# Attention with two key tiles per operation in two double-bank PSUM buffers

## The chip, the cores and the metric

The kernel runs on one core of a Trainium2 chip. Its time is the device time of one launch in microseconds (us); a kernel stands for the median of its runs. TensorE (PE) multiplies matrices into PSUM, VectorE (DVE), ScalarE (ACT) and GpSimd (POOL) do the rest, SyncE (SP) issues most DMAs. Each engine takes its instructions in a fixed order and waits at each for what it needs.

## The reference

One encoder layer on 2048 + 256 tokens of width 1024. The input is normed and projected; eight mLSTM heads and eight attention heads (two key/value heads, head width 64) run side by side; their outputs are projected and added, and a gated feed-forward layer with a width-3 convolution follows. The part that the change touches is the attention:

```python
s = jnp.einsum('bqhgd,bkhd->bhgqk', qi, k).astype(jnp.float32) * scale
p = jax.nn.softmax(s, axis=-1)
return jnp.einsum('bhgqk,bkhd->bqhgd', p.astype(v.dtype), v)
```

Keys are those of the same request: 2048 for the long one, 256 for the short one.

## The kernel before

The program runs in stages: the projections for attention and gates, then attention and mLSTM woven together, then the output projection (`phase_c`, tile `po`), which is woven into the last part of attention, then the feed-forward layer.

**Attention** works in 36 blocks of 512 queries. A block is named by its first head and first query tile of 128: `7_12` is head 7, query tiles 12 to 15. Blocks `0_0` to `7_12` (32 of them) meet 2048 keys, which are 16 key tiles or 8 key pairs `kp`; the four blocks `0_16`, `2_16`, `4_16`, `6_16` belong to the short request and have one key pair. A block goes through these steps:

- `prep` (L494 on) transposes the queries into PSUM (`pq`) and copies them out twice (`qq`, `qm`).
- `maxstep` multiplies 128 queries with 512 keys into a tile `px` (L521), and DVE takes the row maxima (`mx`, L522). A block needs 16 such steps; they are done while the block before it is in its key pairs.
- `prep2` joins the maxima, turns them into a row with TensorE (`pr`, L533), and ACT writes it as row 64 of `qm` (L535), so that a second matmul subtracts the maximum.
- `scores`, for each key tile: two matmuls into `ps` (L544, L545), ACT takes the exponential (`pe`, L548) and copies it rounded into the first half of `xx` (L549), DVE writes the remainder into the second half (L550).
- `values`, two key pairs later (`PLAG`): three matmuls per key tile add into the block's one `pv` bank (L562 to L564). The third takes the remainder from DVE.
- `fin1` copies `pv` out on ACT (`o` L571, `rs` L572, 64 partitions by 512); `fin2` does four reciprocals on DVE (L578), one product on POOL (L579), and stores the block into `mix_d` through POOL's DMA queue (L582).

`px`, `ps`, `pq` and `pr` share one PSUM pool, tag `sc`, of four single-bank buffers (`SCB = 4`). The bank of `pv` has no second buffer. mLSTM has three banks of its own (`mj`/`mv`, and `m` twice).

**What sets the order.** The program is written down as generators that `run_both` draws from in turn by estimated costs; a list scheduler then fixes the order of each engine's instructions by priority and by when it expects each to be ready. So TensorE's order has attention, mLSTM projections and, from 1516 us of the span on, `po` matmuls mixed together. `po` for a group of 256 tokens can only be finished when all heads of those tokens are in `mix_d`: `phase_c` loads them as `cmx` (L918), splits them on ACT and DVE, and multiplies (L932). When attention has ended its buffers go to the feed-forward layer, which begins by loading and combining the normed input (`rn`, `n`, `nt`, L1005 to L1028).

Of the kernel before, what the change touches and what calls it, by code (L numbers as in the profile page):

```python
# [17 lines left out]
P = 128  # L18
# [11 lines left out]
ACOL = 2048  # L30
MPRI = 2000
STORE = "sync"
SCB = 4
MB = 2
MJ = 1
BLK = 768
# [5 lines left out]
NX0 = 2  # L42
NPC = 1
WSTEP = 2
MXE = 4
LASTP = 3
OW3 = 3
OTB = 3
# [20 lines left out]
RW = 4  # L69
PO = 4  # L70
PB = 4
PEB = 3
XB = 6
PLAG = 2
ZT = 3
SG = 3
# [353 lines left out]
def attention(g, tc, s1, s2, pp):  # L430
# [62 lines left out]
    def prep(n):  # L493

        s = HB()
        grp, s.qs, k0, k1 = hbs[n]
        load_q(n)
        load_q(n + 1)
        load_kv(grp, k0, k1)
        s.kv = kv[(grp, k0)]  # L500
        s.nq, s.nk = 4, k1 - k0
        s.N = s.nq * P
        s.nm = "%d_%d" % s.qs[0][0:2]
        qz = qzs.pop(n)
        pq = pp.tile([P, 512], F32R, tag="sc", name="pq" + s.nm)
# [6 lines left out]
        s.mx = sp.tile([P, 4, 4], F32, tag="mx", name="mx" + s.nm, bufs=2)  # L512
        s.nsp = -(-s.nk * P // 512)
        s.todo = [(t, z) for z in range(s.nsp) for t in range(s.nq)]
        return s

    def maxstep(s):
        t, z0 = s.todo.pop(0)
        w = min(512, s.nk * P - z0 * 512)
        ps = pp.tile([P, 512], F32, tag="sc", name=f"px{s.nm}_{t}_{z0}")  # L520
        nc.tensor.matmul(ps[:, 0:w], s.qq[:, t * P:(t + 1) * P], s.kv[z0][0][:, 0:w], start=True, stop=True)  # L521
        nc.vector.tensor_reduce(s.mx[:, t, z0:z0 + 1], ps[:, 0:w], AX.X, ALU.max)  # L522

    def prep2(s):

        nq = s.nq
        s.m4 = sp.tile([P, 4], F32, tag="m4", name="m4" + s.nm, bufs=2)
        nc.vector.tensor_reduce(s.m4[:, 0:nq], s.mx[:, 0:nq, 0:s.nsp], AX.X, ALU.max)
        m4r = sp.tile([P, 4], F32R, tag="m4r", name="m4r" + s.nm, bufs=2)
        nc.vector.tensor_scalar(m4r[:, 0:nq], s.m4[:, 0:nq], -1.0, None, ALU.mult)  # L530
        pr = pp.tile([P, 512], F32, tag="sc", name="pr" + s.nm)
        for t in range(nq):
            nc.tensor.matmul(pr[:, t * P:(t + 1) * P], m4r[:, t:t + 1].to_broadcast([P, P]), g.identr, start=True,  # L533
                             stop=True)
        nc.scalar.activation(s.qm[HD:HD + 1, 0:s.N], pr[HD:HD + 1, 0:s.N], AF.Copy)  # L535

    def scores(s, kp):
        N = s.N
        xs = []
        kk, kl1 = s.kv[kp // 2][0:2]  # L540
        for z in range(2):
            ps = pp.tile([P, 512], F32, tag="sc", name=f"ps{s.nm}_{kp}_{z}")
            kc = (2 * kp + z) % 4 * P
            nc.tensor.matmul(ps[:, 0:N], kk[:, kc:kc + P], s.qq[:, 0:N], start=True, stop=False)  # L544
            nc.tensor.matmul(ps[:, 0:N], kl1[:, kc:kc + P], s.qm[:, 0:N], start=False, stop=True)  # L545
            pe = sp.tile([P, 512], F32, tag="pe", name=f"pe{s.nm}_{kp}_{z}", bufs=PEB)
            x = sp.tile([P, 2, 512], F32R, tag="px", name=f"xx{s.nm}_{kp}_{z}", bufs=XB)
            nc.scalar.activation(pe[:, 0:N], ps[:, 0:N], AF.Exp)  # L548
            nc.scalar.activation(x[:, 0, 0:N], pe[:, 0:N], AF.Copy)  # L549
            nc.vector.tensor_tensor(x[:, 1, 0:N], pe[:, 0:N], f32(x[:, 0, 0:N]), ALU.subtract)  # L550
            xs.append(x)
        return kp, xs

    def values(s, kp, xs):

        N = s.N
# [3 lines left out]
        for z, x in enumerate(xs):  # L560
            kt = 2 * kp + z
            nc.tensor.matmul(s.pv[:, 0:N], vv[:, kt % 4, :], x[:, 0, 0:N], start=kt == 0, stop=False)  # L562
            nc.tensor.matmul(s.pv[0:HD, 0:N], vl[:, kt % 4, :], x[:, 0, 0:N], start=False, stop=False)  # L563
            nc.tensor.matmul(s.pv[:, 0:N], vv[:, kt % 4, :], x[:, 1, 0:N], start=False, stop=kt == s.nk - 1)  # L564

    def fin1(s):

        N = s.N
        s.o1 = sp.tile([HD, 512], F32, tag="o1", name="o1" + s.nm, bufs=2)
        s.rs = sp.tile([HD, 512], F32, tag="rs", name="rs" + s.nm, bufs=1)  # L570
        nc.scalar.activation(s.o1[:, 0:N], s.pv[0:HD, 0:N], AF.Copy)  # L571
        nc.scalar.activation(s.rs[:, 0:N], s.pv[HD:P, 0:N], AF.Copy)  # L572

    def fin2(s):
        N = s.N
        for t in range(s.nq):
            c = slice(t * P, (t + 1) * P)
            nc.vector.reciprocal(s.rs[:, c], s.rs[:, c])  # L578
        nc.gpsimd.tensor_tensor(s.o1[:, 0:N], s.o1[:, 0:N], s.rs[:, 0:N], ALU.mult)  # L579
        for t0, (h, q0, q1) in part(s):  # L580
            r0 = HD * (h % 2)
            nc.gpsimd.dma_start(g.mix_d[q0 // 2:q1 // 2, r0:r0 + HD, 4 + h // 2].rearrange("n p t -> p n t"),  # L582
                           s.o1[:, t0 * P:(t0 + q1 - q0) * P].rearrange("p (n t) -> p n t", t=BT))
            if h == 7:
                g.mixed.update(range(q0, q1))

# [961 lines left out]
```

## Time and profile before

| | |
|---|---|
| median of three runs | 3370.09 us (3361.63 to 3379.33) |
| profiled execution | 3368.61 us, of which 3366.9 us from its first to its last instruction |
| TensorE busy | 97% |
| DVE, ACT, POOL busy | 76%, 60%, 20% |
| mean granted TensorE clock | 0.989 |

Attention begins at about 256 us of the span and ends at about 1773 us. A row of the profile's groups names the line, the engine, the operation, output and input tiles, their shapes and the count; behind the bar stand the busy time in us, the mean duration of one in ns, and the idle time of the engine just before them with what ended it. PEld is TensorE's load of the stationary operand, which overlaps the matmul before it. A matmul's duration covers its passage through the array; the next one can start before it ends, so the distance between two starts is the better price.

### The profile page before, as it was taken

Reading aid. Unit: us, or ns where it says so; the run is one execution under the profiler, and the core shown is the slowest. Engines: PE = TensorE matmul, PEld = TensorE weight load, DVE = VectorE, ACT = ScalarE, POOL = GpSimd, SP = SyncE. Lnnn points to the kernel's source line nnn. Section 1 sums busy time; section 2 is a strip of 40 time slices with the busy share of each in tenths; the row PEclk is TensorE's granted clock in tenths of the full one; section 3 lists DMA queues with packets and bytes.
Section 4 is the critical chain, followed back from the end, with each engine's and each line's share of the span. In section 5 each row is a group of like instructions: output and inputs, shape, how many; then the busy total and the mean of one; then the engine's idle time right before and its main releaser. Section 6 shows DMA issues by size and latency. Waiting matters only on the chain.

```text
span 3366.9 us, 54718 instructions
## 1 busy us (share of the span) xinstructions
PE 3267.3 (97%) x19566; PEld 3033.5 (90%) x19566; DVE 2561.9 (76%) x4259; ACT 2015.5 (60%) x4154; POOL 686.9 (20%) x1040
## 2 busy tenths in 40 slices
PE   7989999999999999999999899999999999999998
PEld 6778888888888888878889899999999999999998
DVE  7875677768767887887775899998888888666663
ACT  4534667666666677666562555666666767554543
POOL 7775123213331332321112000000000000020201
PEclk9999999999999999999999999999999999999999
DMA  8756233333334443434237666668676657867663
GB/s 246 217 181 188 90 103 96 107 106 106 99 106 147 129 124 124 125 106 136 90 102 256 244 216 223 213 241 281 216 247 237 212 191 254 315 230 274 224 236 115
DMA packets 394048, 601.76 MB, mean 179 GB/s; under 512 B 30736, under 2 KB 255024, under 8 KB 393776
## 3 DMA queue, kind: packets, MB, share of 16 engines
q1 hardware_dynamic: 361232, 553.43, 49.2%
q0 software_dynamic: 11088, 33.04, 3.6%
q10 hardware_dynamic: 21456, 11.80, 1.2%
q8 instruction: 154, 2.52, 0.3%
q14 instruction: 118, 0.97, 0.1%
HBM read 434.23 MB, written 163.92 MB: 178 GB/s over the span
## 4 chain that ended last, share of the span: by engine, by line
PE 74%; DVE 7%; issue 5%; DMA 5%; POOL 4%; ACT 4%; SPq 0%; POOLq 0%; ACTq 0%; DVEq 0%
PE pa L1082 16%; PE pc L1082 8%; PE po L932 5%; PE pf L1338 5%; PE pb L1082 4%; PE mj L672 4%; PE mv L682 4%; PE ps L544 3%; PE ps L545 3%; PE pv L564 3%; PE px L521 3%; PE pv L562 3%; PE pv L563 3%; PE pg L1338 2%; PE ph L1338 2%
## 5 line engine op out<-in xcount | busy, mean ns | idle before, releaser
L550 DVE TENSOR_TENSOR xx<-pe,xx 128x512 fp32r<-128x512 f32 x520 | 371.7, 727 | 167.2 <-ACT xx L549 164.1
L548 ACT ACTIVATE pe<-ps 128x512 f32<-128x512 f32 x520 | 299.0, 596 | 153.7 <-PE ps L545 140.6
L522 DVE TENSOR_REDUCE mx<-px 128x1 f32<-128x512 f32 (+1 forms) x528 | 339.0, 669 | 51.3 <-PE px L521 50.0
L1296 POOL TENSOR_TENSOR sq<-sq,sq 128x384 f32<-128x384 f32 x38 | 48.8, 1284 | 1394.9 <-ACT sq L1292 1314.6
L549 ACT ACTIVATE xx<-pe 128x512 fp32r<-128x512 f32 x520 | 316.4, 633 | 4.7
L932 PEld LDWEIGHTS po<-cmx,wo 128*128 128x128 f32 x1728 | 231.5, 190 | 17.8 <-ACT wo L106 0.8
L932 PE MATMUL po<-cmx,wo 128*128 128x256 f32 x1728 | 241.5, 282 | 0.7 <-DVE cx L937 0.3
L1086 ACT ACTIVATE u<-pa 128x386 f32<-128x386 f32 (+2 forms) x264 | 129.2, 490 | 172.1 <-PE pa L1082 171.2
L564 PE MATMUL pv<-xx,vv 128*128 128x512 f32 x520 | 214.5, 413 | 12.3 <-DVE xx L550 12.1
L544 PE MATMUL ps<-qq,kk 128*128 128x512 f32 x520 | 214.3, 415 | 2.0 <-ACT pe L548 1.4
L562 PE MATMUL pv<-xx,vv 128*128 128x512 f32 x520 | 209.8, 403 | 2.3 <-ACT xx L549 1.1
L545 PE MATMUL ps<-qm,kl 65*128 65x512 f32 x520 | 208.5, 404 | 0.1
L563 PE MATMUL pv<-xx,vl 128*64 128x512 f32 x520 | 207.0, 398 | 0.0
L682 PE MATMUL mv<-wm,mn 128*128 128x256 f32 x1296 | 204.9, 287 | 1.9 <-ACT qb L678 1.9
L672 PE MATMUL mj<-mn,wm 128*128 128x256 f32 x1296 | 199.5, 287 | 6.8 <-ACT og L686 4.8
L672 PEld LDWEIGHTS mj<-mn,wm 128*128 128x128 f32 x1296 | 184.1, 191 | 23.7 <-ACT og L686 5.6
L682 PEld LDWEIGHTS mv<-wm,mn 128*128 128x128 f32 x1296 | 187.4, 191 | 18.9 <-ACT qb L678 2.5
L521 PE MATMUL px<-kk,qq 128*128 128x512 f32 (+1 forms) x528 | 199.1, 410 | 3.5 <-ACT qq L509 1.9
L227 PE MATMUL pj<-w_a,n1T 128*128 128x512 f32 (+1 forms) x864 | 178.6, 361 | 10.0 <-DVE n1T L185 6.6
L227 PEld LDWEIGHTS pj<-w_a,n1T 128*128 128x128 f32 x864 | 144.1, 196 | 30.4 <-DVE n1T L185 7.8
L776 ACT ACTIVATE dm<-dm,tm 128x128 f32<-128x128 f32 x288 | 95.7, 392 | 100.4 <-POOL dm L773 95.9
L1082 PE MATMUL pb<-n,wa 128*128 128x386 f32 (+2 forms) x792 | 147.1, 340 | 4.2 <-DVE cx L949 4.2
(322 smaller groups left out, 8375.3 us busy)
## 6 DMA issues: line engine op xcount, KB each, us to landing
mn<-n_d SPq DMA_DIRECT2D x216, 256.0 KB, 3.1
ru<-w_up SPq DMA_DIRECT2D x88, 512.0 KB, 5.1
rs<-wsu_d SPq DMA_DIRECT2D x88, 512.0 KB, 5.6
act_d<-ts SPq DMA_DIRECT2D x33, 768.0 KB, 5.8
nt<-act_d SPq DMA_DIRECT2D x60, 384.0 KB, 5.1
re_t<-wsd_d SPq DMA_DIRECT2D x45, 512.0 KB, 5.2
wsu_d<-tw SPq DMA_DIRECT2D x44, 512.0 KB, 3.6
act_d<-ya SPq DMA_DIRECT2D x99, 192.0 KB, 2.7
```

Of the source, the lines that this page charges most:

```text
L227: nc.tensor.matmul(pjs[t][:, c0:c1], nTs[tiles[t]][:, c, a, :], ws[c][:, b, c0:c1], start=(c == 0 and k == 0), stop=(c == NCC - 1 and k == 2))
L522: nc.vector.tensor_reduce(s.mx[:, t, z0:z0 + 1], ps[:, 0:w], AX.X, ALU.max)
L544: nc.tensor.matmul(ps[:, 0:N], kk[:, kc:kc + P], s.qq[:, 0:N], start=True, stop=False)
L545: nc.tensor.matmul(ps[:, 0:N], kl1[:, kc:kc + P], s.qm[:, 0:N], start=False, stop=True)
L549: nc.scalar.activation(x[:, 0, 0:N], pe[:, 0:N], AF.Copy)
L550: nc.vector.tensor_tensor(x[:, 1, 0:N], pe[:, 0:N], f32(x[:, 0, 0:N]), ALU.subtract)
L562: nc.tensor.matmul(s.pv[:, 0:N], vv[:, kt % 4, :], x[:, 0, 0:N], start=kt == 0, stop=False)
L564: nc.tensor.matmul(s.pv[:, 0:N], vv[:, kt % 4, :], x[:, 1, 0:N], start=False, stop=kt == s.nk - 1)
L672: nc.tensor.matmul(pj[:, o], s.w[c][:, a, o * P:(o + 1) * P], nT[c][:, h, :], start=(c + o + k == 0), stop=(c == NCC - 1 and k == 2 and o ...
L682: nc.tensor.matmul(pv[:, o], nT[c][:, a, o * P:(o + 1) * P], s.w[c][:, h, 256:512], start=(c + o + k == 0), stop=(c == NCC - 1 and k == 2 ...
L932: nc.tensor.matmul(po[:, o], wo[c][z // 2][:, a, n], mx[c][:, h, :], start=(c == 0 and k == 0), stop=(c == NCC - 1 and k == 2))
L1082: s.nc.tensor.matmul(p, w[:, aa, c, :], ops[k][:, c, bb, 0:s.n], start=c == 0 and i == 0 and not add, stop=c == NCC // 2 - 1 and i == 2, s ...
```

## The change

Attention's PSUM pool becomes two buffers of two banks each (`SCB = 2`, tiles of 1024 columns). Everything that goes through it changes shape:

- `maxstep` does two matmuls of 512 keys into one tile and one maximum over 1024 keys. A long block has 8 steps instead of 16. A short block does all four query tiles in one tile and one reduction.
- `scores` puts both key tiles of a pair into one tile by four matmuls; exponential, copy and remainder are one operation each over 1024 columns instead of two over 512.
- `values` reads the halves of the one `xx` tile; its six matmuls are as before.
- `fin1` copies `pv` in four pieces of 64 partitions by 256 columns so that `o1` and `rs` fill 128 partitions by 256; `fin2` then does two reciprocals instead of four, one product over 128 by 256, and two stores per long block instead of one.
- The buffers in SBUF follow: `pe` two of 1024 columns instead of three of 512, `xx` three instead of six. `MXE` goes from 4 to 2, and the table that spaces the maxima at the change of the key/value head is rewritten for 8 steps.

```diff
-SCB = 4
+SCB = 2
-MXE = 4
+MXE = 2
-PEB = 3
-XB = 6
+PEB = 2
+XB = 3
...
     def maxstep(s):
...
+            for z in range(2):
+                nc.tensor.matmul(ps[:, z * 512:(z + 1) * 512], s.qq[:, t0 * P:(t0 + 1) * P], s.kv[2 * z0 + z][0],
+                                 start=True, stop=True)
+            nc.vector.tensor_reduce(s.mx[:, t0, z0:z0 + 1], ps, AX.X, ALU.max)
...
     def scores(s, kp):
...
+        ps = pp.tile([P, 1024], F32, tag="sc", name=f"ps{s.nm}_{kp}")
         for z in range(2):
...
+            nc.tensor.matmul(o, kk[:, kc:kc + P], s.qq, start=True, stop=False)
+            nc.tensor.matmul(o, kl1[:, kc:kc + P], s.qm, start=False, stop=True)
+        pe = sp.tile([P, 1024], F32, tag="pe", name=f"pe{s.nm}_{kp}", bufs=PEB)
+        x = sp.tile([P, 2, 1024], F32R, tag="px", name=f"xx{s.nm}_{kp}", bufs=XB)
+        nc.scalar.activation(pe, ps, AF.Exp)
+        nc.scalar.activation(x[:, 0], pe, AF.Copy)
+        nc.vector.tensor_tensor(x[:, 1], pe, f32(x[:, 0]), ALU.subtract)
...
     def fin1(s):
...
-        nc.scalar.activation(s.o1[:, 0:N], s.pv[0:HD, 0:N], AF.Copy)
-        nc.scalar.activation(s.rs[:, 0:N], s.pv[HD:P, 0:N], AF.Copy)
+        for z in range(2):
+            for r, o in ((0, s.o1), (HD, s.rs)):
+                nc.scalar.activation(o[HD * z:HD * z + HD], s.pv[r:r + HD, 256 * z:256 * z + 256], AF.Copy)
 
     def fin2(s):
-        for t in range(s.nq):
+        for t in range(2):
...
-        nc.gpsimd.tensor_tensor(s.o1[:, 0:N], s.o1[:, 0:N], s.rs[:, 0:N], ALU.mult)
+        nc.gpsimd.tensor_tensor(s.o1, s.o1, s.rs, ALU.mult)
...
-                    k = 2 * (kp - 2) - (nxt.nq * nxt.nsp - len(nxt.todo))
+                    k = (0 if kp < 5 else 2 if kp == 5 else 4) - (nxt.steps - len(nxt.todo))
```

The scheduler gives every engine a new order. Three places of TensorE's order matter below. Names carry block, key pair and a running number; `po4_2` is the output projection of token group 4, `cmx6_7` the attended heads 6 and 7 of token group 6. The changed file is nine lines longer behind the attention, so L932 is L941 there; L544, L545 are L553, L554, and L562 to L564 are L570 to L572.

The first place is block `7_12`, key pairs 6 and 7. Before:

```order
L544 MATMUL ps7_12_6_0_21964<-qq7_12_21541,kk1_16_12_11639 128x512
L545 MATMUL ps7_12_6_0_21964<-qm7_12_21543,kl11_16_12_11640 128x512
L564 MATMUL pv7_12_21869<-xx7_12_4_0_21924,vv1_16_8_11630 128x512
L932 MATMUL po4_2_20832<-cmx4_3_20636,wo3_1_18739 128x256
L544 MATMUL ps7_12_6_1_21972<-qq7_12_21541,kk1_16_12_11639 128x512
L545 MATMUL ps7_12_6_1_21972<-qm7_12_21543,kl11_16_12_11640 128x512
L932 MATMUL po4_2_20832<-cmx4_3_20636,wo3_1_18739 128x256 x2
L544 MATMUL ps7_12_7_0_21986<-qq7_12_21541,kk1_16_12_11639 128x512
L545 MATMUL ps7_12_7_0_21986<-qm7_12_21543,kl11_16_12_11640 128x512
L932 MATMUL po4_2_20832<-cmx4_4_20640,wo4_1_18771 128x256
```

And with the change, from key pair 6 on:

```order
L553 MATMUL ps7_12_6_19929<-qq7_12_19612,kk1_16_12_10655 128x512
L554 MATMUL ps7_12_6_19929<-qm7_12_19614,kl11_16_12_10656 128x512
L572 MATMUL pv7_12_19874<-xx7_12_3_19887,vv1_16_4_10635 128x512
L570 MATMUL pv7_12_19874<-xx7_12_3_19887,vv1_16_4_10635 128x512
L571 MATMUL pv7_12_19874<-xx7_12_3_19887,vl1_16_4_10636 64x512
L572 MATMUL pv7_12_19874<-xx7_12_3_19887,vv1_16_4_10635 128x512
L570 MATMUL pv7_12_19874<-xx7_12_4_19903,vv1_16_8_10646 128x512
L571 MATMUL pv7_12_19874<-xx7_12_4_19903,vl1_16_8_10647 64x512
L553 MATMUL ps7_12_7_19945<-qq7_12_19612,kk1_16_12_10655 128x512
```

No `po` matmul stands there any more: mLSTM and `po` have moved ahead of attention, and from key pair 3 of block `6_12` to the last matmuls of `6_16` (168 rows of the order) attention is alone but for two `po` matmuls near the end.

The second place is the turn from block `6_12` to `7_12`, where `pv` changes hands. Before, the first matmul into the new `pv` stands 20 rows behind the last one into the old, with others of this kind in between:

```order
L564 MATMUL pv6_12_21618<-xx6_12_7_1_21765,vv1_16_12_11641 128x512
L129 MATMUL rs_c3_20710<-ones_82,cacc3_20147 128x2 x2
L521 MATMUL px4_16_1_0_21850<-kk1_2_0_21794,qq4_16_21810 128x256
L932 MATMUL po4_1_20756<-cmx4_0_20624,wo0_0_18708 128x256 x3
L932 MATMUL po4_1_20756<-cmx4_1_20628,wo1_0_18718 128x256 x3
L932 MATMUL po4_1_20756<-cmx4_2_20632,wo2_0_18728 128x256 x3
```

With the change it follows at once:

```order
L570 MATMUL pv6_12_19663<-xx6_12_7_19771,vv1_16_12_10657 128x512
L571 MATMUL pv6_12_19663<-xx6_12_7_19771,vl1_16_12_10658 64x512
L572 MATMUL pv6_12_19663<-xx6_12_7_19771,vv1_16_12_10657 128x512
L570 MATMUL pv7_12_19874<-xx7_12_0_19829,vv1_16_0_10624 128x512
L571 MATMUL pv7_12_19874<-xx7_12_0_19829,vl1_16_0_10625 64x512
```

The bank is the same; what lies between is `fin1`, which is ACT's.

The third place is the end of attention with the change, where `po` is taken up again:

```order
L543 MATMUL pr6_16_20009<-identr_78,m4r6_16_20007 128x128 x4
L553 MATMUL ps6_16_0_20201<-qq6_16_19984,kk1_2_0_19802 128x512
L554 MATMUL ps6_16_0_20201<-qm6_16_19986,kl11_2_0_19803 128x512
L553 MATMUL ps6_16_0_20201<-qq6_16_19984,kk1_2_0_19802 128x512
L554 MATMUL ps6_16_0_20201<-qm6_16_19986,kl11_2_0_19803 128x512
L570 MATMUL pv6_16_20270<-xx6_16_0_20207,vv1_2_0_19804 128x512
L571 MATMUL pv6_16_20270<-xx6_16_0_20207,vl1_2_0_19805 64x512
L941 MATMUL po6_0_20060<-cmx6_7_20052,wo7_0_17149 128x256
L941 MATMUL po6_1_20147<-cmx6_7_20052,wo7_0_17149 128x256
```

Before, `po` of group 5 stands between `pr6_16`, `ps6_16` and `pv6_16`. When attention's last matmul is issued, 1196 of the 1728 `po` matmuls have been issued with the change, and 1037 before it.

More of the change, by code (lines that the diff above doesn't have):

```diff
@@ L504, in prep @@
         qz = qzs.pop(n)
-        pq = pp.tile([P, 512], F32R, tag="sc", name="pq" + s.nm)
+        pq = pp.tile([P, 1024], F32R, tag="sc", name="pq" + s.nm)
         for t in range(s.nq):
@@ L511, in prep @@
         nc.scalar.activation(s.qm[0:HD, 0:s.N], f32(pq[0:HD, 0:s.N]), AF.Copy)
-        s.mx = sp.tile([P, 4, 4], F32, tag="mx", name="mx" + s.nm, bufs=2)
-        s.nsp = -(-s.nk * P // 512)
-        s.todo = [(t, z) for z in range(s.nsp) for t in range(s.nq)]
+        s.mx = sp.tile([P, 4, 2], F32, tag="mx", name="mx" + s.nm, bufs=2)
+        s.nsp = -(-s.nk * P // 1024)
+        s.todo = [(t, z) for z in range(s.nsp) for t in range(s.nq)] if s.nk * P > 512 else [(None, 0)]
+        s.steps = len(s.todo)
         return s
     def maxstep(s):
[L518 to L522, printed above, removed]
+        t0, z0 = s.todo.pop(0)
+        ps = pp.tile([P, 1024], F32, tag="sc", name=f"px{s.nm}_{t0}_{z0}")
+        if t0 is None:
+            w = s.nk * P
+            for t in range(s.nq):
+                nc.tensor.matmul(ps[:, t * w:(t + 1) * w], s.qq[:, t * P:(t + 1) * P], s.kv[0][0][:, 0:w], start=True,
+                                 stop=True)
+            nc.vector.tensor_reduce(s.mx[:, 0:s.nq, 0], ps[:, 0:s.nq * w].rearrange("p (t w) -> p t w", w=w), AX.X,
+                                    ALU.max)
+        else:
+            for z in range(2):
+                nc.tensor.matmul(ps[:, z * 512:(z + 1) * 512], s.qq[:, t0 * P:(t0 + 1) * P], s.kv[2 * z0 + z][0],
+                                 start=True, stop=True)
+            nc.vector.tensor_reduce(s.mx[:, t0, z0:z0 + 1], ps, AX.X, ALU.max)
     def prep2(s):
@@ L530, in prep2 @@
         nc.vector.tensor_scalar(m4r[:, 0:nq], s.m4[:, 0:nq], -1.0, None, ALU.mult)
[L531 removed]
+        pr = pp.tile([P, 1024], F32, tag="sc", name="pr" + s.nm)
         for t in range(nq):
```

40 lines of the change are left out of this document (15 added, 25 removed).

## The prediction

> **What bounds the kernel now.** I read the page first, then the busy time by stage, then what TensorE's weight loads waited for, then the groups of instructions. The page says that TensorE is the busy engine:
>
> ```profile
> span 3366.9 us, 54718 instructions
> PE 3267.3 (97%) x19566; PEld 3033.5 (90%) x19566; DVE 2561.9 (76%) x4259; ACT 2015.5 (60%) x4154; POOL 686.9 (20%) x1040
> ```
>
> By stage (columns: length, then busy time of each engine, granted clock, DMA share, GB/s) attention covers the first three rows, the rest of the output projection and the passage to the feed-forward layer the last two:
>
> ```profile
> 300.00:1000.00 700.00, 691.67 (x4317) 604.08 (x4316) 509.83 (x1071) 468.58 (x1217) 182.73 (x339) 0.99 0.34 104
> 1000.00:1600.00 600.00, 578.22 (x3498) 489.17 (x3497) 472.15 (x1040) 394.88 (x1015) 160.68 (x289) 0.99 0.41 126
> 1600.00:1776.00 176.00, 176.00 (x1165) 157.56 (x1164) 127.32 (x219) 102.28 (x196) 33.31 (x30) 1.00 0.29 95
> 1776.00:1860.00 84.00, 82.89 (x699) 82.43 (x698) 46.42 (x87) 21.69 (x38) 23.17 (x20) 1.00 0.83 279
> 1860.00:1890.00 30.00, 19.42 (x88) 17.66 (x87) 23.41 (x35) 10.10 (x15) 3.94 (x3) 0.83 0.89 304
> ```
>
> In the 1476 us of attention TensorE is idle for 8.3 + 21.8 + 0 = 30 us. DVE is busy for 1109 us (75%) and ACT for 966 us (65%), so neither bounds the stage. What they cost is how often TensorE waits for them. From 255 to 1790 us its weight loads waited like this (us in total, times, longest):
>
> ```profile
> PEld pv L564 <- DVE xx L550: 23.3, 29, 3.0
> PEld px L521 <- ACT pe L548: 4.4, 11, 1.2
> PEld pv L562 <- ACT xx L549: 4.0, 10, 1.0
> PEld ps L544 <- ACT pe L548: 3.4, 7, 1.2
> ...
> PEld px L521 <- DVE mx L522: 2.5, 7, 0.4
> ...
> PEld ps L544 <- DVE mx L522: 2.1, 7, 0.4
> ```
>
> Rows one and three are waits for results, 27.3 us; the other four are waits for a free PSUM buffer, 12.4 us. Together 39.7 us (1.2% of the time) is all that the attention can win by faster ACT and DVE steps.
>
> **The change part by part.** The sum is made against the profiled execution: 3368.61 us, 1.7 us over its span and 1.5 us below the median of the three runs.
>
> The ACT and DVE steps that are merged, and their prices (mean ns of one behind the bar):
>
> ```profile
> L550 DVE TENSOR_TENSOR xx<-pe,xx 128x512 fp32r<-128x512 f32 x520 | 371.7, 727 | 167.2 <-ACT xx L549 164.1 <-PE mv L682 0.6
> L522 DVE TENSOR_REDUCE mx<-px 128x1 f32<-128x512 f32 x512 | 333.0, 677 | 42.4 <-PE px L521 41.2
> L549 ACT ACTIVATE xx<-pe 128x512 fp32r<-128x512 f32 x520 | 316.4, 633 | 4.7
> L548 ACT ACTIVATE pe<-ps 128x512 f32<-128x512 f32 x520 | 299.0, 596 | 153.7 <-PE ps L545 140.6 <-DVE mx L522 4.0 <-DVE xx L550 2.0
> ...
> L578 DVE RECIPROCAL rs<-rs 64x128 f32<-64x128 f32 x144 | 122.5, 901 | 10.3 <-ACT rs L572 9.3 <-POOL rcol_c L133 0.5 <-issue 0.4
> ...
> L1055 DVE TENSOR_TENSOR wa<-ru,wa 128x1024 fp32r<-128x1024 f32 x66 | 80.4, 1222 | 31.5 <-ACT wa L1054 31.4
> ...
> L1054 ACT ACTIVATE wa<-ru 128x1024 fp32r<-128x1024 f32 x66 | 69.5, 1053 | 1.6 <-DMA ru<-w_up 1.6
> ...
> L261 POOL TENSOR_TENSOR t<-xh,tab 128x256 f32<-128x256 f32 x36 | 37.0, 1047 | 11.6 <-DVE xh L249 11.6
> ...
> L678 ACT ACTIVATE qb<-mj 64x256 f32<-64x256 f32 x54 | 20.2, 374 | 0.4
> ```
>
> DVE: the remainder goes from 520 x 0.727 = 378 to 260 x 1.222 = 318 us, -60. The maximum over 1024 has no row; between one old step (0.677, as if width were free) and two (1.354) I take 0.677 plus the growth of the remainder (0.495), 1.17: 512 x 0.677 = 347 to 256 x 1.17 = 300, -47. Reciprocals keep their 128 columns on twice the partitions: 144 to 72 of 0.901, -65. In all -172, so DVE falls from 75% to 63%. ACT: copy 520 x 0.633 = 329 to 260 x 1.053 = 274, -55; exponential likewise, 310 to 260 x 1.016 = 264, -46; `fin1` goes from two steps to four of 64x256, 36 x (4 x 0.374 - 2 x 0.59) = +11. In all -90, 65% to 59%. None of this is on the path by itself: TensorE's work is the same number of matmuls.
>
> POOL's product shrinks from 64x512 to 128x256 (1.05 us at most, above), and some 32 stores are added at 0.645 us of issue each; POOL is busy 20%, and what queues behind a store is mLSTM's `dm`. I cost that at nothing; without the cover it would be 32 x 0.645 = 21 us.
>
> ```profile
> L582 POOL DMA_DIRECT2D mix_d<-o x40 | 25.8, 645 | 7.6 <-POOL o L579 6.5 <-POOL va L687 0.5 <-DVE C L762 0.3
> ```
>
> *Waits for results.* Half as many results are waited for, and DVE's queue is shorter: I halve the 27.3 us, **-14**. The bounds are all of it gone (-27), and each of the 39 waits longer by the 0.495 us that the remainder grows (+19).
>
> The Trainium skill (Perfetto Trace Analysis, section Optimizing Scalar/DVE Operations) speaks for +19: grouping helps an engine that is saturated, but where ACT and DVE aren't saturated and cause bubbles elsewhere, it advises to break steps up. By it the sum below would be 33 us higher. The rows show the premise (75% busy, 29 waits); whether the rule holds here no run has shown yet, and since the scheduler lays TensorE's order to the longer steps I stay with -14 and keep the rule as a rival.
>
> *Waits for a buffer.* There are half as many tiles, in two buffers instead of four, and each is held longer by the growth of the exponential (1.016 - 0.596 = 0.42 us). Below stands all 12.4 us gone, above 260 score tiles each late by 0.42 = 109 us. The order puts new tiles about as far behind the last user of their buffer as before, so I take the low end's neighbourhood, **+5**.
>
> *The end of attention.* This is new work for the clock: 168 rows of the order in which TensorE has only attention. Its price per matmul is read from the chain of waits:
>
> ```profile
> 1704.10 0.47 PE ps L544 x2
> ...
> 1773.30 10.70 PE po L932 x95
> ```
>
> A matmul of 512 columns takes 0.235 us, one of `po` 0.113. The stretch has some 159 of 512 columns, 37.4 us, and small ones for about 3: TensorE needs 40 us. ACT needs in the same stretch 15 x (1.016 + 1.053) = 31 for the pairs, 12 x 0.374 = 4.5 for three `fin1`, and seven steps of about 0.587 (the row below) = 4.1: also 40 us. Two engines with 40 us each and two buffers between them don't overlap wholly. I count three turns of `pv` at 4 x 0.374 + a queue on ACT, 1.7 each, 5; two short blocks whose single pair runs exponential, copy and remainder bare, 2 x 3.3 = 6.6; 13 pairs at 0.3 for an ACT step in front, 4; and the way of the last long block through `mix_d` and `cmx` behind them, 4. Together **+20**, between 0 (full overlap) and +40 (none). Before, the stretch 1600 to 1776 had `po` in these gaps and no idle time at all.
>
> ```profile
> L535 ACT ACTIVATE qm<-pr 1x512 fp32r<-1x512 f32 x36 | 21.1, 587 | 55.6 <-PE pr L533 55.3
> ```
>
> *The passage to the feed-forward layer.* 159 `po` matmuls (1196 - 1037) are done earlier. They are no longer there to cover loads, sums and splits after attention's end, where DMA is busy 83 to 89% and 30 - 19.4 = 11 us are already idle. Between 0 and 159 x 0.113 = +18; most of that chain hangs on the last `po`, which is as far behind as before, so **+3**.
>
> *mLSTM's own waits* on ACT and DVE: both queues get shorter, the steps in them longer; **-3**, between -10 and +10 (from 30 us of idle time in all).
>
> Sum: -14 + 5 + 20 + 3 - 3 = +11; 3368.6 + 11 = 3379.6, so **3380 us**.
>
> **The rivals.**
>
> *The shorter queues win* (faster). The result waits vanish (-27), buffer waits halve (-6), the end costs only 10 because ACT runs ahead there, the passage nothing: -23, 3346 us. For it: DVE sets 29 of the waits and loses 172 us of work. Against it: the end of attention without `po`.
>
> *The big steps and two buffers hold TensorE in the middle* (slower). Scores and maxima take the two buffers in turn; from 300 to 1600 us, whenever ACT or DVE has a mLSTM step in front, the next score tile finds its buffer held and all of TensorE's queue stands, mLSTM included. One pair in three late by 0.42 us is 87 x 0.42 = +36, in place of my +5: 3411 us. It decides from about one pair in nine on (30 x 0.42 = 13 us), where the 0.5% is passed. For it speaks that 32 buffer waits exist with four buffers; against it the order's spacing.
>
> The Trainium skill (Perfetto Trace Analysis, section Optimization Strategy) says that the same gap repeating on the engine that should be saturated can mean too few PSUM buffers, which is what this rival would look like in the trace.
>
> *The end is longer than counted* (slower). In gaps of this kind the granted clock falls, as in the row 1860 to 1890 (0.83); with 40 instead of 20 us lost there: 3400 us.
>
> *Nothing comes of it.* The steps are merged as said, and TensorE's lost time stays the same: 3369 us.
>
> **How the numbers follow.** A measurement of this kernel can tell about 0.5% from no change: 3353 to 3387 us. Chances: forecast 0.40, its own range 3364 to 3396, of which 0.22 lies above 3387 and 0.06 below 3353; shorter queues 0.27, four fifths of it below 3353; two buffers 0.18; longer end 0.08; nothing 0.07. Faster: 0.27 x 0.8 + 0.40 x 0.06 = 0.24. Slower: 0.18 + 0.08 + 0.40 x 0.22 = 0.35. Same: the rest, 0.41. The range leaves out a tenth on each side: the lower third of the faster case, below 3342, and the upper half of the two-buffer case, above 3412.
>
> **What would show it.** Right: DVE near 63% and ACT near 59% of 1476 us; waits of `pv` for DVE's `xx` near 12 us; waits of `ps` and `px` for `pe` and `mx` below 20 us; 15 to 25 us of idle TensorE in the last 60 us of attention, with `pv` waiting for ACT's `rs` at the turns. Wrong: idle TensorE spread over 300 to 1600 us with `ps` or `px` waiting for `pe` or `mx` (two buffers), a remainder waited for longer than 23.3 us (the rule), or no idle time at the end (shorter queues).

## The result, and the profile after

| | before | changed |
|---|---|---|
| median (18 runs each) | 3368.35 us (3360.21 to 3379.33) | 3377.62 us (3372.87 to 3382.29) |
| span of the profiled execution | 3366.9 us | 3378.0 us |
| mean granted TensorE clock | 0.989 | 0.988 |

The changed kernel takes 1.0026 times as long, with an interval of 1.0017 to 1.0035: 9 us slower. The interval leaves out 1, but the difference is less than the half per cent within which the prediction counts a time as the same. The head of the page after the change:

```profile
span 3378.0 us, 53454 instructions
PE 3270.3 (97%) x19566; PEld 3035.8 (90%) x19566; DVE 2453.2 (73%) x3659; ACT 1989.0 (59%) x3706; POOL 692.6 (21%) x1072
```

TensorE does the same 19566 matmuls in nearly the same busy time. DVE is relieved of 109 us. By stage (columns as in the prediction; the attention now reaches to 1803 us):

```profile
300.00:1000.00 700.00, 689.78 (x4400) 607.77 (x4399) 449.84 (x787) 442.20 (x1014) 176.98 (x346) 0.99 0.35 107
1000.00:1600.00 600.00, 584.09 (x3619) 501.97 (x3618) 438.84 (x822) 384.67 (x815) 178.47 (x306) 1.00 0.42 131
1600.00:1740.00 140.00, 136.89 (x862) 119.42 (x861) 88.59 (x114) 70.99 (x100) 23.62 (x24) 0.98 0.29 94
1740.00:1812.00 72.00, 59.51 (x264) 44.05 (x263) 40.39 (x50) 44.45 (x60) 7.28 (x13) 0.91 0.15 44
```

The last row is new: in 72 us at attention's end TensorE is idle for 12.5 us and its clock falls to 0.91. Before, 1600 to 1776 us had no idle time. The waits of TensorE's weight loads from 255 to 1740 us:

```profile
PEld ps L553 <- ACT pe L557: 11.4, 13, 2.0
PEld px L530 <- ACT pe L557: 7.4, 9, 2.1
PEld pv L570 <- ACT rs L580: 7.3, 9, 2.2
PEld pv L570 <- ACT xx L558: 5.7, 8, 1.2
PEld pv L572 <- DVE xx L559: 5.3, 8, 1.1
PEld ps L553 <- DVE mx L532: 4.0, 3, 3.3
...
PEld px L530 <- DVE mx L532: 2.5, 4, 1.3
```

Waits for results (rows four and five) are 11.0 us, before 27.3. Waits for a buffer (rows one, two, six, seven) are 25.3, before 12.4. The turn of `pv`, row three, was 1.8 and is 7.3. Added over all rows of this view, attention's own tiles wait 48.4 us, before 48.1: nothing gained. All other tiles, nearly all mLSTM's, wait 11.6 us, before 22.3. A weight load can wait while the matmul before it still runs, so these sums are larger than TensorE's idle time: from 300 to 1740 us that is 29 us with the change and 30 before.

Where the time went is seen best at equal work. In each trace the matmuls are added up in order, each priced by its kind, and the moment is noted when a given sum is reached. Before reaches one such sum at 1728 us of its span, another at 1927, when attention and output projection are over. The table gives how far another kernel is behind (plus) or ahead (minus) at these two sums, and the difference, which is what the end of attention, with the passage behind it, costs it. The first column moves by about a microsecond with the way the matmuls are priced, by three in the kernel with half-used buffers. The table holds the experiments too. Profiled executions lie up to 7 us from their medians, so the table says where, and the medians say how much.

| kernel | at 1728 | at 1927 | the end | median, us | ratio to before, interval |
|---|---|---|---|---|---|
| changed | -9.7 | +11.8 | 21.5 | 3377.62 | 1.0017 to 1.0035 |
| changed, LEAD 0.7 | -20.0 | +5.1 | 25.1 | 3372.84 | 1.0002 to 1.0020 |
| changed, LEAD 1.0 | -20.2 | +11.6 | 31.8 | 3380.81 | 1.0028 to 1.0055 |
| changed, idle reciprocals | -14.3 | +5.3 | 19.6 | 3376.77 | 1.0014 to 1.0032 |
| changed, maxima split | -13.4 | +9.3 | 22.7 | 3376.15 | 1.0014 to 1.0034 |
| changed, remainder split | -22.6 | -7.5 | 15.1 | 3359.21 | 0.9957 to 0.9982 |
| the same, LEAD 1.0 | -20.0 | +12.8 | 32.8 | 3378.04 | 1.0020 to 1.0042 |
| the same, LEAD 0.7 | -25.0 | +4.6 | 29.6 | 3374.56 | 1.0012 to 1.0029 |
| before, LEAD 1.8 | +10.7 | +22.9 | 12.2 | 3394.45 | 1.0061 to 1.0092 |
| before, two half-used buffers | +196.3 | +233.9 | 37.6 | 3597.69 | 1.0659 to 1.0695 |
| before, new block ends | -21.3 | -18.8 | 2.5 | 3354.19 | 0.9937 to 0.9969 |
| the same, idle reciprocals | -7.8 | -4.6 | 3.2 | 3361.50 | 0.9967 to 0.9986 |
| before, new ends, long SBUF steps | -15.7 | -13.8 | 1.9 | 3356.10 | 0.9953 to 0.9977 |

So the change gains 10 us in the middle and loses 21.5 at attention's end. The seven other kernels of this form gain 13 to 25 us and lose 15 to 33.

What the time consists of can be read at the same two sums, from the gaps between matmuls and from the trace's record of the granted clock, which is 1 or one half. Between the two sums TensorE is idle for 22.6 us where it was 11.7 before, and half clock costs 13.7 us where it cost 5.1 (27.3 us at half clock, before 10.2). Together that is 19.5 of the 21.5 us. From 255 us to the first sum TensorE is idle for 31.1 us where it was 34.5, and half clock costs 10.2 us where it cost 13.7: 7 of the 10.

### The profile page after: what moved, and what is told of

The parts are those of the page before. It is cut to its first block, busy times and chain, and to the rows that moved or that the text cites. A ratio compares the mean times of both kernels' runs of the same rounds, so it can differ in the third digit from the quotient of the medians.

```text
span 3378.0 us, 53454 instructions
## 1 busy us (share of the span) xinstructions
PE 3270.3 (97%) x19566; PEld 3035.8 (90%) x19566; DVE 2453.2 (73%) x3659; ACT 1989.0 (59%) x3706; POOL 692.6 (21%) x1072
## 4 chain that ended last, share of the span: by engine, by line
PE 73%; issue 7%; ACT 5%; DVE 5%; POOL 5%; DMA 4%; SPq 0%; POOLq 0%; ACTq 0%; DVEq 0%
PE pa L1091 16%; PE pc L1091 8%; PE pf L1347 6%; PE po L941 5%; PE pb L1091 4%; PE mj L681 4%; PE ph L1347 3%; PE mv L691 3%; PE ps L553 3%; PE pv L570 3%; PE pv L572 3%; PE ps L554 2%; PE pv L571 2%; PE px L530 2%; PE pg L1347 2%
## 5 line engine op out<-in xcount | busy, mean ns | idle before, releaser
L559 DVE TENSOR_TENSOR xx<-pe,xx 128x1024 fp32r<-128x1024 f32 x260 | 322.9, 1242 | 193.6 <-ACT xx L558 191.9
L557 ACT ACTIVATE pe<-ps 128x1024 f32<-128x1024 f32 x260 | 266.1, 1023 | 225.2 <-PE ps L554 216.2
L532 DVE TENSOR_REDUCE mx<-px 128x1 f32<-128x1024 f32 x256 | 309.8, 1216 | 93.9 <-PE px L530 92.7
L558 ACT ACTIVATE xx<-pe 128x1024 fp32r<-128x1024 f32 x260 | 274.9, 1058 | 6.3 <-PE pv L572 1.3
L941 PEld LDWEIGHTS po<-cmx,wo 128*128 128x128 f32 x1728 | 228.6, 191 | 18.2 <-ACT cmx L928 2.1
L941 PE MATMUL po<-cmx,wo 128*128 128x256 f32 x1728 | 235.8, 283 | 1.4 <-ACT cmx L928 1.1
L553 PE MATMUL ps<-qq,kk 128*128 128x512 f32 x520 | 214.4, 412 | 13.7 <-ACT pe L557 10.4
L570 PE MATMUL pv<-xx,vv 128*128 128x512 f32 x520 | 214.3, 412 | 13.7 <-ACT rs L580 7.8
L572 PE MATMUL pv<-xx,vv 128*128 128x512 f32 x520 | 212.6, 409 | 2.9 <-DVE xx L559 2.8
L554 PE MATMUL ps<-qm,kl 65*128 65x512 f32 x520 | 208.5, 401 | 0.4 <-ACT qm L545 0.4
L691 PE MATMUL mv<-wm,mn 128*128 128x256 f32 x1296 | 192.2, 286 | 0.8 <-ACT qb L687 0.8
L681 PE MATMUL mj<-mn,wm 128*128 128x256 f32 x1296 | 190.2, 288 | 2.8 <-ACT og L695 2.4
L227 PE MATMUL pj<-w_a,n1T 128*128 128x512 f32 (+1 forms) x864 | 179.1, 362 | 10.7 <-DVE n1T L185 6.3
L691 PEld LDWEIGHTS mv<-wm,mn 128*128 128x128 f32 x1296 | 175.9, 190 | 14.1 <-ACT qb L687 1.4
L530 PE MATMUL px<-kk,qq 128*128 128x512 f32 x512 | 165.9, 405 | 5.4 <-ACT pe L557 4.5
L1091 PE MATMUL pc<-nt,wb 128*128 128x386 f32 (+2 forms) x792 | 148.4, 341 | 4.8 <-ACT nt L1015 3.3
```

The costliest lines, as they stand in the source:

```text
L227: nc.tensor.matmul(pjs[t][:, c0:c1], nTs[tiles[t]][:, c, a, :], ws[c][:, b, c0:c1], start=(c == 0 and k == 0), stop=(c == NCC - 1 and k == 2))
L532: nc.vector.tensor_reduce(s.mx[:, t0, z0:z0 + 1], ps, AX.X, ALU.max)
L553: nc.tensor.matmul(o, kk[:, kc:kc + P], s.qq, start=True, stop=False)
L559: nc.vector.tensor_tensor(x[:, 1], pe, f32(x[:, 0]), ALU.subtract)
L570: nc.tensor.matmul(s.pv, vv[:, kt % 4, :], x1, start=kt == 0, stop=False)
L572: nc.tensor.matmul(s.pv, vv[:, kt % 4, :], x2, start=False, stop=kt == s.nk - 1)
```

## The experiments

**Who pays at the end: the form or the lack of other work?** Two kernels change one number of the weaving, and with it the whole order. In the changed kernel, LEAD 0.7 leaves more other work for the end:

```diff
-LEAD = 1.3
+LEAD = 0.7
```

> The changed kernel with one number of the weaving changed (LEAD 0.7 for 1.3: mLSTM is drawn behind attention instead of ahead of it), so that the scheduler leaves other matmuls for attention's end: of TensorE's last 800 instructions up to attention's last, only the last 80 are attention alone, 160 in the changed kernel as it is. My theory (the end costs 21 us because nothing is left to fill it): the end costs 8 to 12 us, idle TensorE in the last 70 us of attention about 6 instead of 12, time about 3367 us (3360 to 3372). Rival (the end's cost belongs to the double-bank form and its two buffers, filler or not): 3375 to 3380 us, and the idle time stands in the same place. If the middle changes by itself, the windows of the trace decide, not the total.

Measured: 3372.84 us, 5 below the changed kernel and just above the range that I gave. The gain is not where I expected it: by the table the end costs 25.1 us, not 8 to 12, and the middle is 10 us better than the changed kernel's. In 20-us stretches from 1740 us on, this kernel first (its attention ends at 1780), then the changed one (ends at 1803):

```profile
1740.00:1760.00 20.00, 20.00 (x120) 17.08 (x119) 16.17 (x26) 16.31 (x23) 4.86 (x6) 1.00 0.18 53
1760.00:1780.00 20.00, 14.95 (x63) 10.33 (x62) 12.49 (x15) 13.52 (x21) 3.70 (x6) 0.88 0.11 27
1780.00:1800.00 20.00, 7.48 (x54) 7.18 (x52) 9.96 (x14) 4.90 (x8) 2.17 (x3) 0.76 0.96 338
1800.00:1820.00 20.00, 18.24 (x138) 18.24 (x139) 8.94 (x13) 4.66 (x7) 4.59 (x4) 0.85 1.04 368
```

```profile
1740.00:1760.00 20.00, 16.95 (x62) 11.49 (x61) 13.63 (x20) 9.05 (x10) 0.10 (x1) 0.83 0.36 113
1760.00:1780.00 20.00, 15.99 (x70) 11.23 (x70) 9.44 (x11) 16.12 (x21) 1.87 (x3) 1.00 0.03 7
1780.00:1800.00 20.00, 15.62 (x71) 11.09 (x69) 12.52 (x14) 16.30 (x23) 2.54 (x4) 1.00 0.05 11
1800.00:1820.00 20.00, 18.95 (x131) 18.24 (x131) 6.51 (x10) 3.61 (x8) 4.25 (x7) 0.83 0.46 127
```

The covered part is full, and the bare part has only 5 us of idle time, with a clock of 0.88. But 12.5 us are idle right behind attention. The waits of the weight loads from 1700 to 1860 us name it:

```profile
PEld po L941 <- DVE cx L946: 14.5, 1, 14.5
PEld pv L570 <- ACT xx L558: 2.8, 1, 2.8
```

`po` waited 14.5 us for the sum that frees its buffer (L946), and that sum for its residual, a load `cx` (L932). In the changed kernel this load was issued by SP from 1705 us on, here from 1794 on:

```profile
L932 SPq DMA_DIRECT2D cx<-xT x8: 327/345/406, 1705.5 to 1752.0; - x8
```

```profile
L932 SPq DMA_DIRECT2D cx<-xT x8: 332/457/1191, 1794.6 to 1818.1; - x8
```

In this order SP has feed-forward's loads `rn` (L1031) ahead of `cx`; they take over attention's SBUF and wait for its last matmul, behind a 30 us wait for a block's store. SP's waits from 1720 to 1830 us:

```profile
SPq L927 <- DMA mix_d<-o: 30.2, 2, 30.0
...
SPq L1031 <- PE pv L572: 4.4, 1, 4.4
```

So the idle time did not stay in the same place, as the rival had it; it moved behind attention, and at the end nothing was saved. The old form with a bare end:

```diff
-LEAD = 1.3
+LEAD = 1.8
```

> The kernel before with LEAD 1.8 for 1.3: the old form, 512 columns and four single-bank buffers, but the scheduler now uses up the other matmuls early and attention's last 160 instructions on TensorE are alone, as in the changed kernel. My theory (a bare end costs, whatever the form): 15 to 20 us more than before, 3383 to 3389 us, with idle TensorE in the last 60 us of attention. Rival (it is the double-bank form that can't run alone; four small buffers overlap): at most 5 us more, 3368 to 3374 us.

Measured: 3394.45 us, 26 more than before and more than either expectation. At equal work it was 11 us ahead at 1546 us of before's span and 23 behind at the end. From 1600 us on:

```profile
1600.00:1740.00 140.00, 128.75 (x670) 102.87 (x669) 103.31 (x173) 84.60 (x157) 14.11 (x13) 0.95 0.19 62
...
1780.00:1800.00 20.00, 17.71 (x78) 12.50 (x77) 14.75 (x23) 16.95 (x33) 2.22 (x2) 1.00 0.03 7
1800.00:1820.00 20.00, 13.24 (x51) 9.17 (x50) 14.61 (x24) 10.45 (x20) 4.55 (x5) 0.77 0.10 26
```

Four single-bank buffers of short steps lose time too when they run alone: by the table 12.2 us at the end, and some 20 more, by the same reckoning, in an earlier stretch, where 205 matmuls of attention stand in a row before 1672 us (in the first row above, 11 us are idle at a clock of 0.95). The rival falls: bare attention costs in either form. Whether it costs more in the double-bank form, 21.5 us against 12.2 at the end, is not settled.

**What do two buffers cost by themselves?**

```diff
-SCB = 4
+SCB = 2
-            ps = pp.tile([P, 512], F32, tag="sc", name=f"ps{s.nm}_{kp}_{z}")
+            ps = pp.tile([P, 1024], F32, tag="sc", name=f"ps{s.nm}_{kp}_{z}")
```

(`px`, `pq` and `pr` likewise; each uses the first 512 columns.)

> The kernel before with its operations of 512 columns unchanged, but in two double-bank buffers of which each tile uses half: the loss of buffers without the larger steps. Attention's last 280 instructions are alone here. My theory (the waits for a buffer, 12.4 us before and 27 after, come from having two buffers): waits of score and maximum tiles for the exponential or the maximum of 25 us or more in the middle, result waits unchanged near 27, and 25 to 35 us more at the end: 3400 to 3415 us. Rival (a buffer is held long only because the steps are long; two buffers of short steps do no harm): buffer waits below 15 us in the middle, only the end is dearer: 3380 to 3390 us.

Measured: 3597.69 us, 229 more than before. From 255 to 1740 us:

```profile
PEld px L521 <- DVE mx L522: 32.8, 56, 2.5
PEld px L521 <- ACT pe L548: 31.7, 73, 1.7
PEld pv L564 <- DVE xx L550: 31.4, 55, 3.1
PEld pv L562 <- ACT xx L549: 21.0, 50, 1.6
PEld ps L544 <- DVE mx L522: 18.5, 42, 1.2
...
PEld ps L544 <- ACT pe L548: 8.9, 25, 1.1
```

The buffer waits are 91.9 us, not 25, and the result waits double as well. This kernel's attention goes on to 2028 us; over the whole of it the buffer waits are 129.3 us and the result waits 70.3, and from 1558 us on six runs of 104 to 201 matmuls are attention alone, so not all of the loss is the middle's. Both theories were wrong in size, the rival in kind: two buffers of short steps do great harm. With 1024 columns used in each, two buffers keep as many score columns in flight as four of 512 did; with 512 used, half as many. That fits the long steps being what makes the change's two buffers bearable; the block ends and the order differ between the two kernels as well.

**What are the new block ends worth alone?** The whole new `fin1` and `fin2` in the kernel before, nothing else:

```diff
-        s.o1 = sp.tile([HD, 512], F32, tag="o1", name="o1" + s.nm, bufs=2)
+        s.o1 = sp.tile([P, 256], F32, tag="o1", name="o1" + s.nm, bufs=2)
...
-        for t in range(s.nq):
+        for t in range(2):
```

> The kernel before with only the ends of blocks changed: pv copied in four pieces of 256 columns, two reciprocals of 128 partitions instead of four of 64, one product, two stores. Scores and maxima stay as before, and so do the four buffers; other matmuls cover attention's end. My theory (DVE's relief of 65 us shortens the waits for the remainder, but the turn of pv is longer by two steps on ACT): -5 to 0 us, 3363 to 3368 us, waits of pv for ACT's rs up from 1.8 to about 6 us. Rival 1 (the reciprocals alone make the gain in the middle): -10 us or more, 3358 us or less. Rival 2 (the longer turn outweighs): 3372 us or more.

Measured: 3354.19 us, ratio 0.9953 (0.9937 to 0.9969): the lowest median of this study. Its waits from 255 to 1740 us:

```profile
PEld pv L564 <- DVE xx L550: 7.7, 12, 2.0
PEld px L521 <- ACT pe L548: 6.5, 9, 1.8
PEld ps L544 <- DVE mx L522: 4.3, 9, 0.7
...
PEld px L521 <- DVE mx L522: 3.6, 10, 0.6
PEld pv L562 <- ACT rs L572: 3.3, 4, 1.5
...
PEld pv L562 <- ACT xx L549: 2.9, 7, 0.8
...
PEld ps L544 <- ACT pe L548: 2.0, 9, 0.3
```

Result waits 10.6 us, buffer waits 16.4: this one part shortens the result waits as much as the whole change does (11.0), without its buffer waits (25.3) and with attention's end covered. The time is rival 1's, and my theory was too modest. To see whether it is DVE's relief, the same kernel and the changed one with the relief taken back:

```diff
+        rd = sp.tile([P, P], F32, tag="rd", name="rd" + s.nm, bufs=1)
+        for t in range(2):
+            nc.vector.reciprocal(rd, s.rs[:, t * P:(t + 1) * P])
```

> The kernel before with the ends of blocks on 128 partitions (3354 us by itself), and behind the two reciprocals of each block two more of the same size into a tile that nobody reads, so that DVE's work in these ends is back at about 130 us while their shape, their stores and TensorE's order stay nearly as they were. Theory (the 14 us gained came from taking 65 us off DVE): the gain goes, 3364 to 3370 us, and the waits of pv for DVE's remainder rise from 7.7 back to 18 us or more. Rival (it came from the shape: a shorter chain at the end of a block, half the product on POOL): 3352 to 3358 us, waits for the remainder below 12 us.

Measured: 3361.50 us, 7 of the 14 us gone; waits for the remainder (L550) up from 7.7 to 12.9 us, not to 18. That fits half of the gain being DVE's time and the other half the shape of the ends, but the order changed with each of these edits, and no run separates it from them. Better founded is that the new ends help: the three kernels that have them in the old form, each in an order of its own, are 7 to 14 us faster than before.

> The changed kernel with the same two idle reciprocals per block, so that DVE does what the old ends of blocks cost it: the two double-bank buffers and long steps without the relief of the reciprocals. If the relief is worth 14 us here too: 3388 to 3396 us, that is, merged scores and maxima by themselves cost 20 us or more. Rival (with the long steps DVE has slack enough and the relief is worth nothing): 3375 to 3382 us.

Measured: 3376.77 us, no different from the changed kernel. The rival's range held: in the double-bank form DVE's 67 us more cost nothing that shows in the time. Its result waits from 255 to 1740 us are 7.6 us, not more than the changed kernel's 11.0. Its middle is 4.6 us better by the table, so another order may hide a small cost.

**Long steps without the loss of buffers.** From the kernel with new ends: exponential per 512 columns out of PSUM, copy and remainder over 1024 in SBUF.

```diff
+            nc.scalar.activation(pe[:, z * 512:(z + 1) * 512], ps, AF.Exp)
+        nc.scalar.activation(x[:, 0], pe, AF.Copy)
+        nc.vector.tensor_tensor(x[:, 1], pe, f32(x[:, 0]), ALU.subtract)
```

> The kernel before with the new ends of blocks, and of the long steps only those that read and write SBUF: the exponential stays at 512 columns out of four single-bank buffers, into halves of one tile; copy and remainder run over 1024 columns. Maxima stay at 512 keys. DVE and ACT lose about 55 us each against the ends alone (3354 us). Theory A (the long steps are good, the loss of PSUM buffers is what costs): 3344 to 3352 us. Theory B (the long steps themselves cost, by making the first half wait for the second): 3358 to 3368 us, with waits for the remainder or the copy up from 10.6 to 18 us or more. Theory C (too little is left to win): 3352 to 3357 us.

Measured: 3356.10 us, the same as the ends alone (3354.19). Theory C: result waits are 15.1 us where they were 10.6, and nothing is won in this order by steps that are cheaper in sum.

**Shorter steps, same buffers.** The changed kernel with the remainder in two halves:

```diff
-        nc.vector.tensor_tensor(x[:, 1], pe, f32(x[:, 0]), ALU.subtract)
+        for z in range(2):
+            c = slice(z * 512, (z + 1) * 512)
+            nc.vector.tensor_tensor(x[:, 1, c], pe[:, c], f32(x[:, 0, c]), ALU.subtract)
```

> The changed kernel with the remainder again in two steps of 512 columns, everything else merged. Rule of the Trainium skill (Perfetto Trace Analysis, Optimizing Scalar/DVE Operations: break steps up where an unsaturated engine causes bubbles): the second matmul on a remainder has it 0.5 us earlier, 3 to 8 us less than the changed kernel, 3369 to 3375 us. Mine: waits for the remainder are only 5.3 us there, while DVE gets 55 us more work: 0 to 8 us more, 3378 to 3386 us.

Measured: 3359.21 us, 18 below the changed kernel and beyond both expectations. But the waits for the remainder hardly moved:

```profile
PEld pv L572 <- ACT rs L582: 7.4, 8, 2.4
PEld pv L574 <- DVE xx L561: 6.0, 9, 1.8
PEld pv L572 <- ACT xx L558: 5.1, 7, 0.9
PEld px L530 <- DVE mx L532: 4.2, 9, 1.1
PEld ps L553 <- ACT pe L557: 3.2, 5, 1.1
```

6.0 us here, 5.3 there. What fell is the wait for the exponential's buffer (`ps`, 11.4 to 3.2), which the split does not touch. That speaks for another order rather than a faster step, so the same edit was made at two other values of LEAD.

> The changed kernel with LEAD 1.0: another order of the same work, whose last 110 rows in attention are alone on TensorE. It stands beside the next run and shows how much an order by itself is worth. If the middle of the changed kernel is an unlucky order (at equal work done it is 10 us ahead of the kernel before, with LEAD 0.7 it was 20): 3364 to 3372 us. If the double-bank form costs that much in every order: 3374 to 3380 us.

> The changed kernel with LEAD 1.0 and the remainder in two steps of 512. Theory A (shorter steps on DVE win by themselves, as the 18 us between the changed kernel and its version with the split remainder say): 10 to 20 us below the same order without the split. Theory B (the split only brought another order, and orders differ by 10 us and more): within 6 us of the run without the split, or above it.

> The changed kernel with LEAD 0.7 and the remainder in two steps of 512, beside 3372.8 us without the split. Theory A (the split wins by itself): 3355 to 3363 us. Theory B (luck of an order): 3367 to 3379 us.

Measured: 3380.81 without and 3378.04 with the split at LEAD 1.0; 3372.84 and 3374.56 at LEAD 0.7. Differences of -18.4, -2.8 and +1.7 us for one edit: theory B. In these two orders the split did shorten the waits for the remainder, from 6.5 to 1.9 us and from 6.0 to 2.5, and yet the time moved by less than 3 us; where the time fell by 18, those waits had not. The order that came with the split at LEAD 1.3 is good in the middle and has the shortest end of all double-bank kernels; the split is not its cause in general. LEAD 1.0 by itself, 3380.81 us, lies just above the second of its two ranges, and for another reason than that range stood for: its middle is 20 us ahead, like that of LEAD 0.7, so the changed kernel's 10 belong to an unlucky order, but its end is dearer. Both kernels with LEAD 1.0 lose 32 us at the end, with `po` waiting 15.5 and 16.4 us for `cx`, like LEAD 0.7 (14.5, and 15.1 with the split).

The maxima in two halves, out of the same tile:

```diff
-            nc.vector.tensor_reduce(s.mx[:, t0, z0:z0 + 1], ps, AX.X, ALU.max)
+            for z in range(2):
+                nc.vector.tensor_reduce(s.mx[:, t0, 2 * z0 + z:2 * z0 + z + 1], ps[:, z * 512:(z + 1) * 512], AX.X, ALU.max)
```

> The changed kernel with the two halves of each tile of maxima reduced in two steps of 512 keys, all else merged, the buffers as they are. Theory A (long steps on DVE stand before the remainder that TensorE waits for; shorter ones win): 3360 to 3370 us, waits for the remainder below 5 us. Theory B (what is held is the buffer, and it is held as long by two short steps as by a long one; DVE gets 35 us more): 3376 to 3384 us.

Measured: 3376.15 us, with the changed kernel's 3377.62 inside what the runs can tell. Waits for the remainder 7.5 us. Theory A falls; the split costs nothing measurable either.

## Why the prediction was right, point by point

The forecast of 3380 us and its sign held, and so did the main step, a loss at attention's end that is larger than the gain in the middle. But the parts did not all come out as counted, and some errors cancelled. That the time lies within 2.4 us of the forecast is luck: the eight kernels of this form, which differ in order and in small edits, lie between 3359 and 3381 us, one of them outside the range of 3364 to 3396.

- **DVE and ACT.** DVE was to fall by 172 us of the 1476, to 63%, ACT by 90, to 59%. Measured in the same stretch: DVE 1109 to 998 us (68%), ACT 966 to 919 (62%). The direction holds, the size was too large. The maximum had no row; it took 1.216 us, not 1.17. The remainder took 1.242, not 1.222:

```profile
L559 DVE TENSOR_TENSOR xx<-pe,xx 128x1024 fp32r<-128x1024 f32 x260 | 322.9, 1242 | 193.6 <-ACT xx L558 191.9
L532 DVE TENSOR_REDUCE mx<-px 128x1 f32<-128x1024 f32 x256 | 309.8, 1216 | 93.9 <-PE px L530 92.7
L585 DVE RECIPROCAL rs<-rs 128x128 f32<-128x128 f32 x72 | 63.3, 920 | 19.5 <-ACT rs L580 19.4
```

  And count times mean overstates busy time: the old remainder was 520 x 0.727 = 378 by that product, 371.7 by its row, since neighbours overlap a little. The rows of attention's steps give 833 - 701 = -132. The rest of the way to -111 is other work that now falls into the stretch.
- **Waits for results, -14.** Measured 27.3 to 11.0, -16.3. Right in size. The two reasons given don't add up, though: the new block ends alone bring these waits to 10.6, and the merged steps with DVE's relief taken back to 7.6.
- **Waits for a buffer, +5.** Measured +12.9, to 25.3; the mark of "below 20 us" was missed. In other orders of the same form they were 16.1 (LEAD 0.7) and 14.9 (LEAD 1.0), so part of it is the order. It is the two-buffer rival's mechanism at a third of its price, but not by its count: the waits are not more, 29 after 32 before, but longer, 0.87 us each after 0.39. The longest, 3.3 us up to 1642.7 us, was for a maximum that stood on DVE behind eight steps of `cx` (L958, of the output projection) and a block's two reciprocals; from 1643.4 us on 6.8 us at half clock followed.
- **The turn of `pv`.** Counted at the end of attention only; in the middle the weight loads wait 5.5 us more for it, and the sum had no term for it there.
- **mLSTM's own waits, -3.** Measured 22.3 to 11.6, -10.7, outside the bounds of -10 to +10, while in attention's own tiles -16.3 + 12.9 + 5.5 and small rows come to nothing. That this is about the gain of the middle, -9.7, does not make it its cause: at equal work TensorE's idle time fell by 3.4 us only, and 3.5 us are clock, a term that the sum did not have.
- **The end of attention, +20.** Measured 21.5, but of another make. All four parts of the +20 were idle time; measured are 10.9 us more of it and 8.6 us of clock, which the forecast put at nothing and only a rival named. The match in size is luck. In 1740 to 1812 us the idle time is 12.5 us, and the clock fell to half twice, for 6.8 us each (below). The mark said 15 to 25 us idle in the last 60; it was 3.05 + 4.01 + 4.38 = 11.4. `pv` waited for `rs` at two turns there, 4.1 us, of the 5 counted for three. And the first of the idle time is not due to attention's own steps alone. From the chain of waits:

```profile
1740.61 2.32 DMA cmx<-mix_d
1742.95 0.42 ACT cmx L928
...
1744.96 2.79 DVE cx L958 x8
...
1748.01 1.23 DVE xx L559
```

  The exponential whose buffer TensorE waited for stood on ACT behind a split of `cmx` that itself waited for its load, and the next remainder stood on DVE behind eight steps of `cx`. TensorE had all but run out of `po`, but ACT and DVE still had other steps of the output projection, and these came first. The prediction had no term for that.
- **The passage, +3.** Measured 0 in the changed kernel: by the reckoning of the table it is as far behind at 1850 us of before's span as at 1927 and long after, +11.8 to +12. In the four kernels with LEAD 1.0 and 0.7 the loss shows just there, as 14.5 to 16.4 us, near the +18 given as the upper bound, but as a wait for one late load.
- **The rule on long steps** (the Trainium skill, Perfetto Trace Analysis, section Optimizing Scalar/DVE Operations) gave a sum 33 us higher. The remainder is waited for 5.3 us where it was 23.3, so the longer step did no such harm. Splitting it again shortened these waits in two orders of three, and the time clearly in the third alone.
- **Rivals.** The shorter queues' -23 failed at the end of attention. The longer end needed 40 us; it took 21.5, though the falling clock that it names was there. That two buffers can hold TensorE is shown by the kernel with half-used buffers; there the reading of the Trainium skill (Perfetto Trace Analysis, section Optimization Strategy: a gap that repeats can mean too few PSUM buffers) agrees with the trace, 129.3 us of buffer waits beside 229 us lost.

What stays open is why the scheduler leaves so little for the end. All eight kernels of the changed form had 1196 `po` matmuls done before attention's last matmul, which uses up token groups 0 to 5; before it were 1037, with the new ends alone 863. The old form with LEAD 1.8 and the kernel with half-used buffers stop at the same 1196, so this count is where `po` runs out and not a mark of the long steps. Attention's last matmul comes at 1803 us, 1772 and 1730. That longer steps make the scheduler place attention later and other work in between fits this, but was not tested by itself. A kernel that holds `po` back for the end was not tried either.

## What to carry to other kernels

Price a change of several parts part by part on the chip: here one part alone was 14 us faster, and merged with the others it was 9 us slower. Where two streams are woven, ask how much of the filling stream is left when the bounding stream ends, what steps of it stand ahead on the other engines, and in which order the loads of the next stage stand on their queue; that decided more here than the price of any step. And where a scheduler lays out a new order for every edit, make the same edit in two or three orders before believing a difference of 10 to 20 us.

## What the runs showed of the hardware

- A reciprocal over 128 columns takes 0.901 us on 64 partitions and 0.920 on 128: twice the partitions are almost free.
- A maximum over 1024 columns in PSUM takes 1.216 us, over 512 columns 0.677, over 256 columns 0.415: about 1.05 ns per column and 0.14 us fixed.
- TensorE's clock can fall to half after a gap of under 2 us. In the changed kernel a score tile's weight load waited 1.9 us for its buffer up to 1744.3 us (1.7 us without any matmul); from 1745.8 to 1752.4 us the chain then shows matmuls of 512 columns at 0.43 us, before and after them at 0.23:

```profile
1740.35 0.24 PE ps L554
...
1750.50 0.43 PE pv L571
...
1752.93 0.24 PE ps L553
```

  The granted clock in 1745 to 1750 us is 0.58 and in 1750 to 1755 us 0.74. The Trainium skill (TensorE: Matmul & The Clock Gate, section on the HAM clock gate) says that the array goes to half its clock after an idle window of about 3.4 us; here a wait of 1.9 us was enough. It is not the only place: in the kernel before, 1.88 us without a matmul up to 936.5 us were followed by a granted clock of 0.57 in 937 to 941 us. But 1.74 us without one, up to 1025.4 us, were followed by no clock below 1.00 up to 1032 us, so the length of the gap alone does not decide. In the traces' record of the clock each fall between 255 and 1930 us lasts 3.4, 6.8 or 10.2 us, in both kernels.
